# When a planned two-layer decoder trunk emits its weight loads, its reloads of x and the users of rows read back from DRAM

## The chip, the cores and the metric

The kernel runs on one core of one Trainium2 chip, as one program. The metric is the device time of one execution in microseconds (us); lower is better. Every time below is from the runs of the kernel before the change, or from one execution of it that the hardware profiler recorded.

## The reference

The reference is a decoder trunk of two layers over 256 positions of width 2048, all in float32. Each layer normalises its input, multiplies it by one wide input projection (`w_in`), feeds four groups of heads from the columns, gates each group, concatenates the four and multiplies by `w_out`; the result is added to x.

```python
h = rms_norm(x, norm_g)
p = split_columns(jnp.einsum("bsd,de->bse", h, w_in))
fox  = forgetting_attention(...) * silu(p["fox_g"])       # softmax with a cumulative forget bias
diff = rms_norm(differential_attention(...)) * silu(p["diff_g"])   # difference of two softmaxes
moba = moba_attention(...) * silu(p["moba_g"])            # at 256 positions: one causal block
gla  = rms_norm(gla_chunked(...)) * silu(p["gla_g"])      # gated linear attention
mixed = jnp.concatenate([fox, diff, moba, gla], axis=-1)
return x + jnp.einsum("bse,ed->bsd", mixed, w_out)
```

After the second layer comes one more rms_norm.

## The kernel before

**Products in parts.** Every weight tile is split into a high part (ScalarE, ACT, rounds it to the matmul's format) and a low part (VectorE, DVE, subtracts the high part from the raw tile). The activations are kept in two parts as well, `hTp` (layer input, transposed) and `mTh`, `mTl` (mixed rows, transposed). TensorE (PE) adds three products for each tile: high by high, low by high, high by low.

**Steps.** The work is a list of steps, `plan`. A plain step is two tiles of 128 rows by 512 columns, one raw load of 512 KB, and 12 matmuls; some blocks are 348 columns wide. Two of the input projections, `moba_v` and `diff_v`, are computed together in seven products of half size, the forms p1 to p7; their pair steps have 6 matmuls, and take a raw tile, or a tile `y` that lives in the buffer `xs` and is summed up in DRAM-to-SBUF transfers. `xs` holds x otherwise, so x is read back into it later, in four chunks of 512 columns: from the input in layer 0, from a copy in DRAM (`kept`) in layer 1. `X_AFTER` gives the steps after a layer's last pair step at which the four reloads are issued. The last pair step lies three steps into the block `diff_g`; `moba_g` follows with eight steps, and then `w_out`.

**Buffers.** There are five raw buffers and four for each of the high and low parts. A raw buffer is free when its low part has been computed.

**Order.** Nothing is scheduled by the hardware beyond the order in which instructions are written into each engine's queue, and semaphores. The order is made when the program is built, by a loop over the steps (lines 1706 to 1754). In each pass, for step i: results of finished blocks are taken (`settle`); `prepare(i + 3)` writes the high part of the step three ahead; the x reload stands here, if there is one; the matmuls of step i are written; `tick()` lets side tasks (attention, transposes, norms, written as generators) write some of their instructions; and `complete(i + 3)` writes the low part. The loads of raw tiles are written by `load_more()`, at the end of `prepare` and `complete`, as long as one of five buffers counts as free. Before the change a buffer counts as free as soon as its low part has been written into DVE's queue. The load itself carries the wait for that low part, and it stands in the queue of SyncE (SP), which issues in order.

**Estimates.** To decide when a side task may go on, the builder keeps a clock of its own, `times.now`, that the matmuls advance, and an estimated end for every tile. A task that yields goes on in a pass where the end of what it last wrote is at most `LEAD` = 1.5 us ahead of that clock; up to three such turns fit in one pass. Ends include a `HANDOVER` of 0.2 us. If a task yields a number, it goes on only when the clock has reached that end plus the number. These estimates decide order alone; at run time only the queues and semaphores count.

**Rows through DRAM.** A transposition of 128 x 1024 values is done in two moves, `turned`: DVE transposes 32 x 32 squares (STREAM_TRANSPOSE), SP writes the tile to DRAM in four transfers (`far<-four`, line 273), GpSimd (POOL) reads it back in another order (`four<-far`), and ACT copies it into place (`four<-four`). The estimate for the writes is `WRITE` = 5 us, for the read `READ` = 7.5. Queries, keys, probabilities and some gates go this way, and so do chunks of the layer input and the mixed rows of the groups `gla` and `diff` before `w_out`. In `w_out` the groups are used in the order gla, fox, diff, moba; PE's first step with diff rows is step 26 after the last pair step.

The lines that matter in the profile: L267 is any ACT or DVE instruction with an estimate, L273 a transfer with one, L442 a matmul, L1405 a raw load of a plain step, L1369 one of a pair step, L1366 a load of y, L1720 an x reload.

Of the kernel before, what the change touches and what calls it, by code (L numbers as in the profile page):

```python
# [34 lines left out]
RAW_BUFS = 5  # L35
PART_BUFS = 4
WARM = (512,) * 7 + (256,)
HALVED = 3
X_AFTER = (4, 10, 16, 22)
MIDDLE = ("gla_v", "fox_q", "fox_k", "fox_v", "fox_g", "diff_q", "diff_k", "moba_q", "moba_k", "diff_g", "moba_g", "moba_v", "diff_v")  # L40
NAMES = ("moba_v", "diff_v")
PAIR = tuple(3 + MIDDLE.index(z) for z in NAMES)
# [11 lines left out]
STALL = 0.3  # L54
LEAD = 1.5
HANDOVER = 0.2
SAFE = 1.0
ROOM = 2.0
BEFORE_LO = 1.5
# [190 lines left out]
class Timed:  # L250
# [5 lines left out]
    def __getattr__(self, name):  # L256
        f = getattr(self.eng, name)

        def call(*args, **kw):
# [4 lines left out]
            for a in (args[0], kw.get("accum_out")):  # L264
                if a is not None:
                    self.times.end(a, self.tail + HANDOVER)
            return f(*args, **kw)  # L267
# [72 lines left out]
def hybrid_trunk(  # L340
# [18 lines left out]
    times = Times()  # L359
# [23 lines left out]
    def take_side():  # L383
        yield SAFE
        return (yield from side.take([P, 1024]))

    def take_both():
        yield SAFE
        while len(side.free) < 2:
            yield  # L390
        return [side.get([P, 1024]) for _ in range(2)]
# [46 lines left out]
    def matmul(out, lhsT, rhs, start, stop, tiles=1, **kw):  # L438
        n = int(np.prod(rhs.shape[1:]))
        times.now += (n * 4 if lhsT.dtype == F32 else n + 32) / 2400.0 / tiles  # L440
        times.end(out, times.now + HANDOVER)
        t_.matmul(out, lhsT, rhs, start=start, stop=stop, **kw)  # L442

    def transpose(out, src):
        times.now += 0.109
        times.end(out, times.now + HANDOVER)
        t_.transpose(out, src, ident)
# [16 lines left out]
    def turned(pool, srcs, drop, what):  # L464


        x = sum(z.shape[2] for z in srcs)
        t = yield from pool.take([P, x * P])
        to, at = t.rearrange("p (j x r) -> p j x r", j=4, r=32), 0
        for z in srcs:  # L470
            v_.transpose(to[:, :, at:at + z.shape[2]], z)
            at += z.shape[2]
        drop()
        yield
        d = yield from far.take([4, 32, 4, x * 32])
        for i in range(4):
            q_.move(d[:, :, i].rearrange("j c f -> c j f"), t[32 * i:32 * i + 32].rearrange("c (j f) -> c j f", j=4), WRITE)
        yield
        g_.move(t, d.rearrange("j c i f -> (j c) (i f)"), READ)
        far.put(d)  # L480
        yield
        return t, t.rearrange("p (i x r) -> p x i r", i=4, r=32)

    def squares(rows):
# [863 lines left out]
    for i, s in enumerate(plan):  # L1348
        if "pair" in s:
            orders += [("y", i, None)] * (s["form"] == FORM_ORDER[0]) + [("raw", i, q) for q in s["from"]]  # L1350
        else:
            orders.append(("raw", i, None))
    loads = {"next": 0, "out": 0}

    def load_x(eng, a, b):
        if a % 4 == 0:
# [7 lines left out]
    def load_pair(kind, s, q):  # L1364
        if kind == "y":
            nc.sync.dma_start(ys[:, s["c"]], chunk_of(s, ("12", s["c"])))  # L1366
            return
        raw = wst.tile([P, STEP_W], F32, name="raw", bufs=RAW_BUFS).rearrange("p (j c) -> p j c", j=2)
        nc.sync.dma_start(raw, chunk_of(s, q))  # L1369
        s.setdefault("raws", []).append(raw)  # L1370

    def load_more():
        while loads["next"] < len(orders):
            kind, i, q = orders[loads["next"]]
            s = plan[i]
            if kind == "raw" and loads["out"] == RAW_BUFS:
                return
            if kind == "y" and s["pair"] and "kept" not in ready:
                return
            if "pair" in s:  # L1380
                load_pair(kind, s, q)
            else:
                load(i)
            loads["out"] += kind == "raw"
            loads["next"] += 1
            s["here"] = s.get("here", 0) + 1

# [145 lines left out]
    def rest_of_form(s):  # L1533
        l, f, c = s["pair"], s["form"], s["c"]
        y, raw = ys[:, c], s["raws"][0] if s["from"] else None
        lo_of(s["lo"], s["src"], s["hi"])
        if BY_DMA:
            q = {FORM_ORDER[0]: "11", "p5": "22", "p7": "21"}.get(f)
            if q:
                at = where[l, (q, c)]  # L1540
                g_.move(y, weights[at:at + P * 1024].rearrange("(p j c) -> p j c", p=P, j=2), 9.5, accum_op=OP.add)
        elif f == "p1":
            v_.tensor_add(y, y, raw)
        loads["out"] -= len(s["from"])

    def multiply_form(s):
        l, f, c = s["pair"], s["form"], s["c"]
# [84 lines left out]
    def prepare(i):  # L1632
        if i == 3:
            split_xt((2, 3))
        if 5 < i < 24 and i % 6 < 2:
            split_xt([i // 6 * 4 + i % 6 * 2 + k for k in range(2)])
        if i < len(plan):
            s = plan[i]
            while s.get("here", 0) < (len(s["from"]) + (s["form"] == FORM_ORDER[0]) if "pair" in s else 1):
                tick(False)  # L1640
                load_more()
            (form_parts if "pair" in s else parts_of)(s)
            soon = plan[i + 1] if i + 1 < len(plan) else {}
            if soon.get("form") == "p7" and "raws" in soon and "summed" not in soon:
                sum_early(soon)
        load_more()

    def complete(i):
        if i < len(plan):
            s = plan[i]  # L1650
            if "pair" in s:
                rest_of_form(s)
            else:
                if i >= HALVED:
                    lo_of(s["lo"], s["raw"], s["hi"])
                loads["out"] -= 1
            load_more()

    banks = {"next": deque(range(4)), "s": None}
# [1 line left out]
    def settle(waiting, bank=None):  # L1661

        tries = PATIENCE
        while waiting:
            if waiting[0]["key"] not in ready or len(s4.free) <= (KEPT if tries else 0):
                if bank is None or all(bank not in b["banks"] for b in waiting):
                    return
                tick(False)
                tries = max(tries - 1, 0)
                continue  # L1670
            b = waiting.popleft()
            times.latest = 0.0
            b["done"](results(b))
            if b["aside"]:
                side.put(b["side"])
# [8 lines left out]
    def lasts(z):  # L1684
        return 1.36 if "pair" in z else len(z["kts"]) * (z["block"]["n"] + 32) / 400.0
# [3 lines left out]
    last_of = {l: max(i for i, s in enumerate(plan) if s.get("pair") == l) for l in range(DEPTH)}  # L1689
    x_at = {last_of[l] + k: (l, c) for l in range(DEPTH) for c, k in enumerate(X_AFTER)}  # L1690
    load_more()
# [14 lines left out]
    for i, s in enumerate(plan):  # L1706
        if ("r", 0) not in ready:
            next(rms, None)
        while results_of:
            pair_result(results_of.popleft())  # L1710
        if banks["s"] is not None and "done" in pairs[banks["s"]]:
            banks["next"].append(pairs[banks["s"]]["bank"])
            banks["s"] = None
        settle(waiting)
        prepare(i + ahead)
        if i in x_at:
            l, k = x_at[i]
            c = slice(k * 512, k * 512 + 512)
            src = kept.rearrange("p (m d) -> p m d", m=2)[:, :, c] if l else x[0, :, c].rearrange("(m p) c -> p m c", p=P)
            nc.sync.dma_start(xs[:, :, c], src)  # L1720
        while not s["need"] <= ready.keys():
            tick(False)
        if "pair" in s:
            if s["form"] == FORM_ORDER[0] and s["first"]:
                k, ps = take_bank(False)
                pairs[s["pair"]] = {"bank": k, "ps": ps}
                banks["s"] = s["pair"]
            s["ps"] = pairs[s["pair"]]["ps"]
            multiply_form(s)
            if s["last"]:  # L1730
                results_of.append(s)
            if s["last"] and s["form"] in SUM_OF:
                given_out(("paired", s["pair"], SUM_OF[s["form"]]))
            if s["last"] and s["form"] == "p4":
                pairs[s["pair"]]["done"] = True
        else:
            b = s["block"]
            if s["first"]:
                b["banks"] = ()
                if b["aside"]:  # L1740
                    b["side"] = side.get([P, 1024])
                    b["ps"] = [b["side"][:, m * 512:m * 512 + 512] for m in range(2)]
                else:
                    b["banks"], b["ps"] = zip(*[take_bank() for _ in range(2)])
            multiply(s)
            if s["last"] and b["done"]:
                waiting.append(b)
        soon = sum(lasts(z) for z in plan[i + 1:i + ahead])
        ranks["v"] = min(AHEAD, soon - BEFORE_LO)
        ranks["a"] = min(AHEAD, soon - BEFORE_HI, ROOM if s["last"] else AHEAD)  # L1750
        tick()
        ranks["v"] = ranks["a"] = AHEAD
        complete(i + ahead)
    while tasks:
        tick(False)
    b = plan[-1]["block"]
# [31 lines left out]
```

## Time and profile before

| | |
|---|---|
| median of 3 runs | 908.04 us (906.04 to 908.85) |
| the profiled execution | 906.93 us, span 905.2 us |
| PE busy | 885.9 us (98%) |
| DVE busy | 662.6 us (73%) |
| ACT busy | 558.7 us (62%) |
| mean granted clock of PE | 0.995 |
| moved by DMA | 227.45 MB, mean 251 GB/s |
| raw loads of 512 KB | 271, median 5.3 us from issue to landing |

The profile shows each instruction with its engine and line, and for each idle stretch of an engine what ended it. "A <-B" after a duration is such a wait. The span runs from the first to the last instruction; busy time is the union of the instructions' times, and for PE it is modelled, so that a busy PE may still run at a reduced clock. "SPq" is SP's queue, which does nothing but issue transfers.

### The profile page before, as it was taken

Reading aid. Unit: us, or ns where it says so; the run is one execution under the profiler, and the core shown is the slowest. Engines: PE = TensorE matmul, PEld = TensorE weight load, DVE = VectorE, ACT = ScalarE, POOL = GpSimd, SP = SyncE. Lnnn points to the kernel's source line nnn. Section 1 sums busy time; section 2 is a strip of 40 time slices with the busy share of each in tenths; the row PEclk is TensorE's granted clock in tenths of the full one; section 3 lists DMA queues with packets and bytes.
Section 4 is the critical chain, followed back from the end, with each engine's and each line's share of the span. In section 5 each row is a group of like instructions: output and inputs, shape, how many; then the busy total and the mean of one; then the engine's idle time right before and its main releaser. Section 6 shows DMA issues by size and latency. Waiting matters only on the chain.

```text
span 905.2 us, 12467 instructions
## 1 busy us (share of the span) xinstructions
PE 885.9 (98%) x4380; PEld 752.4 (83%) x4380; DVE 662.6 (73%) x943; ACT 558.7 (62%) x846; POOL 60.4 (7%) x87
## 2 busy tenths in 40 slices
PE   9999999999999999989999989999999999999996
PEld 7988889888888888878899867898888888887786
DVE  6679988788677856657559947968767679565673
ACT  7567675587546658555746856657755466594561
POOL 1000110010010000000000010110001100001000
PEclk9999999999999999999999999999999999999999
DMA  8889997669797585968778997768959966859742
GB/s 295 277 264 309 257 303 234 225 193 317 231 290 243 192 296 191 321 229 249 253 242 297 292 324 199 217 194 287 290 213 272 290 215 200 303 180 352 267 153 94
DMA packets 84142, 227.45 MB, mean 251 GB/s; under 512 B 9979, under 2 KB 30443, under 8 KB 83950
## 3 DMA queue, kind: packets, MB, share of 16 engines
q1 hardware_dynamic: 73336, 192.00, 62.6%
q0 software_dynamic: 9152, 33.03, 14.0%
q10 hardware_dynamic: 1590, 1.62, 0.5%
q8 instruction: 34, 0.56, 0.2%
q14 instruction: 30, 0.25, 0.1%
HBM read 204.06 MB, written 22.55 MB: 250 GB/s over the span
## 4 chain that ended last, share of the span: by engine, by line
PE 81%; DMA 7%; DVE 5%; issue 5%; ACT 1%; POOL 0%; POOLq 0%; SPq 0%; ACTq 0%; DVEq 0%
PE mm L442 70%; PE side L442 11%; DMA four<-far 3%; DMA raw<-in_weights 2%; DVE lo L267 2%; DMA far<-four 1%; DVE four L267 1%; DVE mx L267 1%; DVE tq L267 0%; DVE mTl L267 0%; ACT hi L267 0%; ACT four L267 0%; ACT mTh L267 0%; DMA neg_b<-in_const_b 0%; DVE side L267 0%
## 5 line engine op out<-in xcount | busy, mean ns | idle before, releaser
L442 PE MATMUL mm<-hi,hTp 128*128 128x512 f32 (+1 forms) x1760 | 432.3, 382 | 3.7 <-ACT hi L267 3.1
L267 ACT ACTIVATE hi<-raw 128x1024 fp32r<-128x1024 f32 (+2 forms) x319 | 317.2, 1009 | 190.9 <-PE mm L442 110.6
L267 DVE TENSOR_TENSOR lo<-raw,hi 128x1024 fp32r<-128x1024 f32 (+2 forms) x319 | 363.3, 1155 | 94.0 <-ACT hi L267 87.6
L442 PEld LDWEIGHTS mm<-hi,hTp 128*128 128x128 f32 x1760 | 323.1, 188 | 64.1 <-ACT hi L267 4.3
L442 PE MATMUL mm<-lo,hTp 128*128 128x512 f32 (+1 forms) x880 | 237.9, 380 | 1.3 <-DVE lo L267 1.3
L442 PEld LDWEIGHTS mm<-lo,hTp 128*128 128x128 f32 x880 | 162.5, 188 | 33.1 <-DVE lo L267 3.4
L442 PE MATMUL mm<-hi,mTh 128*128 128x512 f32 (+1 forms) x256 | 70.0, 380 | 5.2 <-ACT mTh L267 5.2
L442 PE MATMUL mm<-lo,mTh 128*128 128x512 f32 (+1 forms) x256 | 69.7, 379 | 0.5 <-DVE lo L267 0.5
L442 PE MATMUL mm<-hi,mTl 128*128 128x512 f32 (+1 forms) x256 | 70.0, 381 | 0.1
L442 PEld LDWEIGHTS mm<-hi,mTh 128*128 128x128 f32 x256 | 45.8, 189 | 13.9 <-ACT mTh L267 6.0
L442 PEld LDWEIGHTS mm<-lo,mTh 128*128 128x128 f32 x256 | 46.6, 190 | 10.3 <-DVE lo L267 1.4
L442 PEld LDWEIGHTS mm<-hi,mTl 128*128 128x128 f32 x256 | 46.7, 190 | 9.7 <-DVE mTl L267 0.9
L267 ACT ACTIVATE four<-mm,rstd 128x512 f32<-128x512 f32 (+2 forms) x56 | 36.6, 669 | 25.1 <-PE mm L442 25.0
L273 POOL DMA_DIRECT2D four<-far x40 | 22.4, 559 | 406.2 <-DMA far<-four 175.1
L267 ACT ACTIVATE four<-four 128x512 fp32r<-128x512 f32 (+3 forms) x44 | 35.1, 820 | 18.2 <-DMA four<-far 18.1
L267 DVE STREAM_TRANSPOSE four<-four 128x1024 f32<-128x1024 f32 (+1 forms) x34 | 38.4, 1138 | 0.1
L442 PEld LDWEIGHTS side<-four,four 128*128 128x128 f32 (+1 forms) x336 | 36.3, 190 | 2.4 <-issue 1.4
L442 PE MATMUL side<-four,four 128*128 128x128 f32 (+3 forms) x336 | 37.2, 281 | 0.0
L273 POOL DMA_DIRECT2D xs<-in_weights x24 | 21.0, 875 | 208.5 <-DVE lo L267 55.0
L267 DVE TENSOR_TENSOR mTl<-four,mTh 128x1024 fp32r<-128x1024 f32 x16 | 19.5, 1220 | 17.7 <-ACT mTh L267 17.7
L267 ACT ACT_TABLE_LOAD x22 | 28.2, 1283 | 5.4 <-DVE nb L267 5.1
L267 DVE TENSOR_TENSOR four<-four,four 128x512 fp32r<-128x512 f32 (+3 forms) x31 | 26.6, 881 | 6.3 <-ACT four L267 6.3
(146 smaller groups left out, 679.2 us busy)
## 6 DMA issues: line engine op xcount, KB each, us to landing
raw<-in_weights SPq DMA_DIRECT2D x271, 512.0 KB, 5.3
four<-far POOLq DMA_DIRECT2D x34, 512.0 KB, 7.1
far<-four SPq DMA_DIRECT2D x128, 128.0 KB, 5.0
raw<-in_weights SPq DMA_DIRECT2D x46, 348.0 KB, 4.4
xs<-in_weights POOLq DMA_DIRECT2D x24, 512.0 KB, 7.6
xs<-in_weights SPq DMA_DIRECT2D x8, 512.0 KB, 7.9
xs<-in_x SPq DMA_DIRECT2D x4, 512.0 KB, 5.7
kept<-xs SPq DMA_DIRECT2D x1, 2048.0 KB
```

The lines of the kernel that those rows point to most:

```text
L267: return f(*args, **kw)
L273: self.eng.dma_start(out, src, **kw)
L442: t_.matmul(out, lhsT, rhs, start=start, stop=stop, **kw)
```

## The change

Three things are changed.

- **Loads.** `load_more` no longer takes a buffer as free when its low part is written, but when that low part's estimated end is at most `SOON` = 0.5 us ahead of the builder's clock. The ends wait in a queue, `loads["freed"]`. `load_more` is called at three more places of the loop: after `settle`, after the matmuls and before `tick`, and after `complete`. Where `prepare` needs a load that has not been written, it writes it at once (`urgent`).
- **Reloads of x.** `X_AFTER` goes from (4, 10, 16, 22) to (14, 18, 22, 26).
- **Rows from DRAM.** The last `yield` of `turned` becomes `yield LANDED`, with 0.01, so that the task goes on when the clock has reached the estimated landing.

```diff
-X_AFTER = (4, 10, 16, 22)
+X_AFTER = (14, 18, 22, 26)
...
+SOON = 0.5
+LANDED = 0.01
...
         g_.move(t, d.rearrange("j c i f -> (j c) (i f)"), READ)
         far.put(d)
-        yield
+        yield LANDED
...
-    loads = {"next": 0, "out": 0}
+    loads = {"next": 0, "out": 0, "freed": deque()}
...
-    def load_more():
+    def load_more(urgent=False):
+        by = math.inf if urgent else times.now + SOON
         while loads["next"] < len(orders):
             kind, i, q = orders[loads["next"]]
             s = plan[i]
-            if kind == "raw" and loads["out"] == RAW_BUFS:
+            if kind == "raw" and loads["out"] == RAW_BUFS and not (loads["freed"] and loads["freed"][0] <= by):
                 return
...
-            loads["out"] += kind == "raw"
+            if kind == "raw" and loads["out"] == RAW_BUFS:
+                loads["freed"].popleft()
+            else:
+                loads["out"] += kind == "raw"
...
     def rest_of_form(s):
...
-        loads["out"] -= len(s["from"])
+        loads["freed"].extend([times.of(s["lo"])] * len(s["from"]))
...
     def prepare(i):
...
                 tick(False)
-                load_more()
+                load_more(True)
...
     def complete(i):
...
-                loads["out"] -= 1
+                loads["freed"].append(times.of(s["lo"]))
             load_more()
...
         settle(waiting)
+        load_more()
         prepare(i + ahead)
...
             multiply(s)
             if s["last"] and b["done"]:
                 waiting.append(b)
+        load_more()
         soon = sum(lasts(z) for z in plan[i + 1:i + ahead])
...
         tick()
         ranks["v"] = ranks["a"] = AHEAD
         complete(i + ahead)
+        load_more()
```

## The prediction

> **What bounds the kernel now.** I read the page first, then the waits of TensorE, then windows around those waits, then the queues there.
>
> ```profile
> span 905.2 us, 12467 instructions
> PE 885.9 (98%) x4380; PEld 752.4 (83%) x4380; DVE 662.6 (73%) x943; ACT 558.7 (62%) x846; POOL 60.4 (7%) x87
> ```
>
> TensorE (PE) is busy for 98% of the span; the change alters no arithmetic, so only PE's idle time and its slow time can be won. The waits of PE (engine, line, what ended the wait: us in total, times, longest) say where:
>
> ```profile
> PE mm L442 <- ACT mTh L267: 5.2, 2, 2.9
> PE mm L442 <- ACT hi L267: 3.1, 1, 3.1
> PE mm L442 <- DVE lo L267: 1.8, 6, 0.4
> ```
>
> Ten microseconds in all, three waits making up 8.3. The windows (length, busy us and instructions of PE, PEld, DVE, ACT, POOL; granted clock; DMA share, GB/s) add what follows them:
>
> ```profile
> 370.00:380.00 10.00, 10.00 (x46) 8.29 (x45) 7.92 (x8) 4.86 (x7) 0.54 (x1) 1.00 1.03 370
> 392.00:394.00 2.00, 2.00 (x6) 1.52 (x6) 2.00 (x4) 2.00 (x4) 0.00 (x0) 0.54 0.36 119
> 530.00:540.00 10.00, 7.08 (x32) 5.53 (x30) 2.43 (x7) 2.92 (x3) 2.00 (x3) 1.00 1.04 367
> 542.00:544.00 2.00, 2.00 (x6) 1.52 (x6) 1.76 (x8) 2.00 (x4) 0.00 (x0) 0.50 0.71 248
> 550.00:560.00 10.00, 9.07 (x38) 6.47 (x37) 9.83 (x23) 5.87 (x8) 1.74 (x2) 1.00 0.66 160
> 840.00:850.00 10.00, 9.96 (x54) 8.63 (x55) 5.86 (x7) 5.80 (x7) 0.00 (x0) 1.00 0.87 328
> ```
>
> After the waits near 388 and 538 us the granted clock is about 0.5 for some 3.5 us (the rows at 392 and 542), which costs about 1.7 us each; after the third, near 837, it stays 1.00. So three places hold at most 8.3 + 3.4 us, plus about a microsecond of DVE-bound time at 550.
>
> **The change, part by part.** No instruction is added or removed; order in the queues changes. Part one, the loads: SP stands at a raw load, waiting for the low part that frees its buffer, for most of the kernel:
>
> ```profile
> SPq L1405 <- DVE lo L267: 527.4, 241, 8.6
> ```
>
> Whatever SP was given behind such a load waits too. Where only raw loads stand in the queue, emitting them later changes nothing: each still goes when its buffer is free. It matters only where row writes (far<-four, line 273) stand behind. Part three, `LANDED`: the ACT copy of rows read back from DRAM is emitted only at the estimated landing, not up to 1.5 us (`LEAD`) before, so more high parts go ahead of it on ACT. Where ACT waits for a late landing, nothing behind the copy is held that could have run; where the estimate was right, the consumer comes up to a step later.
>
> *Place A, 531 to 545 us (layer 1 begins).* PE, then ACT:
>
> ```profile
> 528.76 1.07 PE L442 MATMUL mm<-hi,hTp 128*128 128x512 f32 x4
> 530.12 1.98 PE L442 MATMUL mm<-hi,hTp 128*128 128x512 f32 x8
> 532.84 1.98 PE L442 MATMUL mm<-hi,hTp 128*128 128x512 f32 x8
> 535.56 1.07 PE L442 MATMUL mm<-hi,hTp 128*128 128x512 f32 x4
> 540.20 3.45 PE L442 MATMUL mm<-hi,hTp 128*128 128x512 f32 x8 [3.12 <-ACT hi L267]
> 544.65 1.99 PE L442 MATMUL mm<-hi,hTp 128*128 128x512 f32 x8
> ```
> ```profile
> 532.01 1.06 ACT L267 ACTIVATE hi<-raw 128x1024 fp32r<-128x1024 f32 x1 [4.14 <-DMA raw<-in_weights]
> 538.14 1.06 ACT L267 ACTIVATE four<-four 128x1024 f32<-128x1024 f32 x1 [5.07 <-DMA four<-far]
> 539.11 1.04 ACT L267 ACTIVATE hi<-raw 128x1024 fp32r<-128x1024 f32 x1
> 540.05 2.44 ACT L267 ACTIVATE four<-ct,dgs 128x128 f32<-128x128 f32 x8
> 542.39 2.00 ACT L267 ACTIVATE hi<-raw 128x1024 fp32r<-128x1024 f32 x2
> ```
>
> A plain step takes 532.84 to 535.56 = 2.72 us, a pair step half of it, so PE wanted the high part of 539.11 at 536.92 and began at 540.20: 3.28 us lost. The step then took 4.45 us (540.20 to 544.65), 1.73 over, the clock. ACT was not short of work: it stood behind the copy of 538.14. That copy was emitted between two high parts, in the pass that ends at PE's 530.12; that the pass before, at 528.76, did not emit it puts its estimated landing between 530.3 and 531.6 (1.5 us after each), so at 530.12 the new rule does not yet hold and the copy goes one step later, behind the high part of 539.11. Were that one's weights there? The rows on the way:
>
> ```profile
> 505.23 1.24 DVE L267 STREAM_TRANSPOSE four<-four 128x1024 f32<-128x1024 f32 x1
> 514.02 4.96 SPq L1405 DMA_DIRECT2D raw<-in_weights  x3
> 519.51 2.13 SPq L273 DMA_DIRECT2D far<-four  x4
> 523.83 4.57 SPq L1405 DMA_DIRECT2D raw<-in_weights  x3
> 531.33 0.55 POOL L273 DMA_DIRECT2D four<-far  x1 [9.97 <-DMA far<-four]
> ```
>
> They were issued by 523.83; even at the 11.8 us that the writes took (519.51 to 531.33) they land by 535.6, and the high part ends by 536.7. PE then starts at 536.92. The next high part follows the copy, 538.14 + 1.06 + 1.04 = 540.2, against 539.64 wanted; so that step begins near 540.2 instead of 544.65, a gain of 4.45, and with the eight small copies (2.44) ahead of the next high part some 3.8 is left a step later. Then it is given back in part: everything else behind the copy on ACT comes only one high part (1.05 us) earlier, and DVE, which from 541 on works off what ACT hands it (9.83 busy of 10 in the window at 550, PE 9.07), sets the pace. Ends: −5.0 (3.28 + 1.73, all kept) and +2.7 (a consumer one step late). Between the 1.05 that ACT surely passes on and 3.8, I take −2.0, nearer the ACT row because DVE follows ACT. That the writes go ahead of a raw load helps at most by the last load of the 514.02 row, about 1.5 us; I count nothing, since DVE's backlog also held back their emission.
>
> *Place B, the two layer ends.* The chain of waits with the timeline of layer 0, and below it layer 1:
>
> ```profile
> 360.28 16.35 PE mm L442 x72
> ...
> 379.32 8.19 DMA four<-far
> ```
> ```profile
> 367.40 1.24 DVE L267 STREAM_TRANSPOSE four<-four 128x1024 f32<-128x1024 f32 x1
> 367.55 3.14 SPq L1405 DMA_DIRECT2D raw<-in_weights  x2
> 369.10 2.37 DVE L267 TENSOR_TENSOR lo<-raw,hi 128x1024 fp32r<-128x1024 f32 x2 [0.46 <-ACT hi L267]
> 370.74 2.17 SPq L273 DMA_DIRECT2D far<-four  x4
> 389.82 1.57 PE L442 MATMUL mm<-hi,mTh 128*128 128x512 f32 x4 [2.31 <-ACT mTh L267]
> ```
> ```profile
> 819.84 2.27 SPq L273 DMA_DIRECT2D far<-four  x4
> 838.78 1.20 PE L442 MATMUL mm<-hi,mTh 128*128 128x512 f32 x4 [2.85 <-ACT mTh L267]
> ```
>
> The diff group's mixed rows are transposed by 368.64, but SP stands at the second load of the 367.55 row until its low part ends, about 370.3, and the writes start at 370.74: 2.1 us late, on the very chain (write, read 8.19, copy, high part) that PE waits for. Layer 1 repeats it. Does the new rule let the writes go first? Between two passes only the step's matmuls move the planner's clock (2.72); the load call behind them takes the load if its low part's estimated end lies within 2.72 + 0.5 = 3.22 us of the old pass; else the row writes, emitted next, precede it. From the transpose's start to that low part's end the trace has 2.94 us; `HANDOVER` adds 0.2; and that the writes were not emitted in the transpose's own pass says it started over 0.16 us after the planner's clock (1.34 + lag > 1.5). Sum 3.30 against 3.22: the writes go first, narrowly. Then they start 2.1 us earlier and the load about 0.5 us later, which its low part's three-step lead covers. What is late next is the read itself, so −2.1 of the 2.31 in layer 0 and −2.1 of the 2.85 in layer 1. Ends: layer 0 −4.0 (with the clock), layer 1 −2.85, and +2.7 each if the chain loses a step instead.
>
> On the clock, rows first: 0.54 after a wait of 2.31, 1.00 after one of 2.85. The Trainium skill, page "TensorE: Matmul & The Clock Gate", section "The HAM clock gate", says that the clock halves after an idle window of about 3.4 us that runs free of the program; no wait here is that long, so by the rule nothing would be won on the clock, by the row of 392 another 1.7. I count nothing.
>
> Part two, the x reloads: eight transfers of the same size, later on SP.
>
> ```profile
> 326.14 0.40 SPq L1720 DMA_DIRECT2D xs<-in_x  x1
> ...
> 343.57 1.06 ACT L267 ACTIVATE four<-four 128x1024 f32<-128x1024 f32 x1 [3.44 <-DMA four<-far]
> ...
> 345.12 2.84 PE L442 MATMUL side<-four,four 128*128 128x128 f32 x24
> ```
>
> The first stood ahead of the diff probabilities' writes; without it their read lands sooner and ACT's 3.44 us shrinks. But PE reached the product at 345.12 without waiting, so the order of PE's program sets it: cost and gain 0. The new places are steps 14, 18, 22 and 26, counted from the last pair step; step 26 is the one that PE waits for at 389.82, and the 360.28 row holds steps 16 to 21, so from about 354 to 390 there is one transfer more than before (at 16 and 22); ends −0.5 and +1.5 at place B (the issue, and 512 KB at the 370 GB/s of the 370 window), I take 0, since the row at 370 is as full either way.
>
> **Sum.** −2.0 − 2.1 − 2.1 = −6.2. The profiled execution took 906.93, so 900.7; the median of the runs, 908.04, is 1.1 above it, so 901.8.
>
> **The rivals.** *Nothing moves:* DMA share is 1.03 and 1.04 at the places, and order among transfers makes no bandwidth; then the reads land as late as now and only part of A is left, 0 to −2: 906 to 908. For it speaks the 11.8 us that the writes took; against it, that a load of 512 KB would stand behind 512 KB of writes and not ahead. The Trainium skill, page "DMA: Bandwidth & Descriptors", section "Issuing engines are not separate DMA queues", says that transfers of all issuing engines interleave on the same 16 DMA engines; by that only SP's 2.1 us of standing could be won, and at full share not even that. *Only one place gains:* A alone −2 to −4, or B alone −4.2: 904 to 906. *Slower:* `LANDED` delays the copy of 343.57 past one more step. Its product then comes 2.72 us later in PE's order, the diff rows with it, and both layer ends wait 2.7 us longer, with a second clock loss of 1.7: 5.4 + 1.7 − 2.0 = +5.1, so 913. It decides at an estimated landing later than the pass that now takes it, and 1.51 of a step's 2.72 is 0.55 were nothing known; but ACT's wait of 3.44 shows the estimate to be early, and the gain of 2.1 at place B would offset part of it.
>
> **How the numbers follow.** Both places gain: 0.42, 897 to 904 (either place by 2 us more or less). One place: 0.22, half of it beyond the 0.3% (2.7 us) that a measurement of this kernel can tell from no change. Nothing: 0.16. Slower: 0.20, a tenth of it offset to no change. So faster 0.55, same 0.26, slower 0.19. The range leaves 0.05 below (all ends of A and B at once, −11.5, 896.5) and some 0.13 above 911.
>
> **What would show it.** Right: ACT's order at place A has the copy behind one more high part and PE's wait there is under 1 us with the clock at 1.00; at the layer ends the writes start within 0.2 us of the transpose's end, ahead of the load, and PE waits below 1 us. SP's wait for low parts changes little in total. Wrong: the read at the layer ends is issued as late as now, or the product of 345.12 moves a step later; or new waits of PE for low parts near 550, where DVE has no room. It would also fail if copies emitted later left row buffers held so long that other tasks start late.

## The result, and the profile after

| kernel | median, us | lowest to highest | span of the profiled execution, us | mean granted clock |
|---|---|---|---|---|
| before | 907.04 | 903.87 to 908.85 | 905.2 | 0.995 |
| after | 895.81 | 895.38 to 896.36 | 893.6 | 0.998 |

The ratio is 0.988, with a 95% interval of 0.985 to 0.9911: 11 us, nearly twice the 6.2 us that the prediction summed to, and below its range.

First the page of the kernel after, span and busy time:

```profile
span 893.6 us, 12483 instructions
PE 881.4 (99%) x4380; PEld 751.4 (84%) x4380; DVE 662.7 (74%) x943; ACT 558.7 (63%) x846; POOL 60.4 (7%) x87
```

The same 4380 matmuls take 4.5 us less of busy time (885.9 before), 3.4 of them because two stretches at half clock, 3.4 us each, are gone, and PE is idle for 12.2 us instead of 19.3 (span less busy time). That is the 11.6 us of the span. The waits of PE after (engine, line, what ended the wait: total us, times, longest):

```profile
PE mm L444 <- DVE lo L269: 2.6, 5, 1.3
PE mm L444 <- ACT four L269: 1.4, 1, 1.4
```

The three waits of before (2.31, 3.12 and 2.85 us, for `mTh` twice and for `hi`) are gone; one of 1.4 us for an eviction (ACT takes a finished block from the matmuls' accumulators, `four<-mm`) and one of 1.3 for a low part are new. The windows (length, busy us and instructions of PE, PEld, DVE, ACT, POOL; granted clock; DMA share, GB/s) at the places of before:

```profile
370.00:380.00 10.00, 10.00 (x46) 8.29 (x45) 8.00 (x8) 5.25 (x7) 0.54 (x1) 1.00 1.02 378
392.00:394.00 2.00, 2.00 (x11) 1.65 (x10) 2.00 (x4) 1.16 (x2) 0.00 (x0) 1.00 0.89 263
530.00:540.00 10.00, 10.00 (x46) 8.29 (x45) 7.68 (x20) 8.12 (x15) 0.55 (x1) 1.00 1.04 362
542.00:544.00 2.00, 2.00 (x10) 1.67 (x9) 0.27 (x1) 1.99 (x4) 0.29 (x1) 1.00 0.53 61
```

PE is full in all four, the clock is 1.00 where it was 0.54 and 0.50, and the DMA share at 370 and 530 is as high as before: the transfers have no more room there.

The end of layer 0 in the timeline after (start, us, engine, line, operation, what it waited for), by queue: DVE, SP, POOL, ACT, PE, and below it two rows of the end of layer 1:

```profile
367.49 1.24 DVE L269 STREAM_TRANSPOSE four<-four 128x1024 f32<-128x1024 f32 x1
...
368.75 2.10 SPq L275 DMA_DIRECT2D far<-four  x4
370.95 1.41 SPq L1411 DMA_DIRECT2D raw<-in_weights  x2
...
377.16 0.54 POOL L275 DMA_DIRECT2D four<-far  x1 [11.64 <-PE mm L444]
...
384.38 1.15 ACT L269 ACTIVATE four<-four,dng 128x1024 f32<-128x1024 f32 x1 [3.92 <-DMA four<-far]
385.56 1.06 ACT L269 ACTIVATE mTh<-four 128x1024 fp32r<-128x1024 f32 x1
...
387.81 1.07 PE L444 MATMUL mm<-hi,mTh 128*128 128x512 f32 x4
```
```profile
809.11 2.10 SPq L275 DMA_DIRECT2D far<-four  x4
...
817.40 0.53 POOL L275 DMA_DIRECT2D four<-far  x1 [10.60 <-DMA far<-four]
```

The writes start at 368.75, 0.02 us after their transpose ends (367.49 + 1.24), and the raw load that stood ahead of them goes at 370.95, behind them. `mTh` is ready at 386.62, 1.2 us before PE wants it. The next lines show the place where layer 1 begins (SP, POOL, ACT, PE):

```profile
510.02 4.64 SPq L1411 DMA_DIRECT2D raw<-in_weights  x2
514.72 1.93 SPq L275 DMA_DIRECT2D far<-four  x4
516.74 0.42 SPq L1411 DMA_DIRECT2D raw<-in_weights  x1
517.20 0.50 SPq L1368 DMA_DIRECT2D xs<-in_weights  x1
...
522.11 0.55 POOL L275 DMA_DIRECT2D four<-far  x1 [5.28 <-DMA far<-four]
...
531.28 1.06 ACT L269 ACTIVATE hi<-raw 128x1024 fp32r<-128x1024 f32 x1 [0.20 <-DMA raw<-in_weights]
532.25 1.04 ACT L269 ACTIVATE four<-four 128x1024 f32<-128x1024 f32 x1
...
535.86 1.98 PE L444 MATMUL mm<-hi,hTp 128*128 128x512 f32 x8
```

Here two transfers of 512 KB that were ahead of the writes, a raw load and the `y` load (`xs<-in_weights`), are behind them. From the first write to the read's issue, which this document calls the way of the writes, it takes 7.4 us (514.72 to 522.11) instead of 11.8, and ACT's copy of 532.25 waits for nothing.

Comparing when the same matmul starts in both traces tells where the time came from (positive: after is ahead):

| stretch | change of the lead, us |
|---|---|
| start to 370 us | −0.5 |
| end of layer 0, 390 us | +4.2 |
| beginning of layer 1, 540 us | +5.2 |
| 619 to 637 us | −1.3 |
| end of layer 1, 838 us | +3.5 |

That is 11.1 of the 11.6 us; the rest lies in the rows behind the last of these matmuls. The first row is hardly the work of the change: two kernels below that hold none of its three parts, with `y` put later and with the row writes issued by POOL, are 0.8 and 1.7 us behind at 370 us as well.

### The profile page after: what moved, and what is told of

It reads as the page before. It is cut to its first block, busy times and chain, and to the rows that moved or that the text cites. A ratio compares the mean times of both kernels' runs of the same rounds, so it can differ in the third digit from the quotient of the medians.

```text
span 893.6 us, 12483 instructions
## 1 busy us (share of the span) xinstructions
PE 881.4 (99%) x4380; PEld 751.4 (84%) x4380; DVE 662.7 (74%) x943; ACT 558.7 (63%) x846; POOL 60.4 (7%) x87
## 4 chain that ended last, share of the span: by engine, by line
PE 92%; DVE 3%; DMA 1%; ACT 1%; issue 1%; POOLq 0%; POOL 0%; DVEq 0%; SPq 0%; ACTq 0%
PE mm L444 78%; PE side L444 14%; DVE lo L269 1%; DMA raw<-in_weights 1%; DVE mx L269 1%; DVE side L269 1%; ACT four L269 1%; DMA four<-in_xt 0%; DVE four L269 0%; ACT hi L269 0%; DVE tq L269 0%; ACT L269 0%; DVE mTl L269 0%; ACT mTh L269 0%; POOLq L1793 0%
## 5 line engine op out<-in xcount | busy, mean ns | idle before, releaser
L269 DVE TENSOR_TENSOR lo<-xs,hi 128x1024 fp32r<-128x1024 f32 x24 | 29.2, 1215 | 4.2 <-ACT hi L269 4.2
```

## Experiments: which part does it

Theory after the result: the loads' rule makes the whole gain, at each of the three places by putting one load behind the row writes. Rivals: `LANDED` makes the gain where layer 1 begins (540 us in the table); the x reloads, which leave the queue ahead of the layer ends, make the gain there; or the finer spacing of all loads does. The first kernels switch the three parts.

**The loads' rule alone**: the kernel after, without the other two parts.

```diff
-X_AFTER = (14, 18, 22, 26)
+X_AFTER = (4, 10, 16, 22)
...
-        yield LANDED
+        yield
```

> The load change alone (x reloads and row copies as before). Theory 1 (the order on SP makes the layer ends, the later copies make place A): the row writes start within 0.2 us of their transpose's end at both layer ends and PE's waits there go, 4.2 us in layer 0 and 3.5 in layer 1, while place A (layer 1's begin) keeps its wait of 3.1 us: about 899 us against 907. Rival 1 (the x reloads make the layer ends): the two waits stay, about 907. Rival 2 (place A is made by the row writes and their read coming earlier too): all three waits go, about 895.

Measured: 895.55 us, ratio 0.9862 (0.9823 to 0.9901). TensorE has no wait above 0.8 us:

```profile
PE mm L444 <- DVE lo L269: 2.7, 7, 0.8
```

All three waits are gone with this part alone, as its second rival had it; the lead grows by 4.3 at the end of layer 0, 4.3 where layer 1 begins and 3.5 at the end of layer 1.

**The x reloads alone**: the kernel before with the new `X_AFTER`.

```diff
-X_AFTER = (4, 10, 16, 22)
+X_AFTER = (14, 18, 22, 26)
```

> The x reloads alone (loads and row copies as before). Theory 1: nothing, 906 to 908, since PE's order sets the product of the diff rows, and SP still stands at the load ahead of the row writes at the layer ends. Rival 1: the layer ends gain 2 us or more each, 900 to 903.

Measured: 908.38 us, ratio 1.0001 (0.9981 to 1.002). All three waits stay (4.5 us for `mTh` in two, 3.5 for `hi`). The reloads neither help nor cost.

**LANDED alone**: the kernel before with the last `yield` of `turned` changed.

```diff
-        yield
+        yield LANDED
```

> The later row copies alone (loads and x reloads as before). Theory 1: place A gains 4 to 5 us because the copy on ACT stands behind one more high part, the layer ends keep 2.3 and 2.85 us: about 902. Rival 2: the read lands as late as before (about 6 us behind its estimate), so the copy still stands in front of the next high part and place A gains 2 us or less: 905 to 907. Slower, 910 or more, if the product of the diff rows slips by a step.

Measured: 906.13 us, ratio 0.9971 (0.9943 to 0.9999), barely a gain. Its timeline, ACT and then PE, and below it two rows of the kernel before:

```profile
535.37 1.06 ACT L268 ACTIVATE hi<-raw 128x1024 fp32r<-128x1024 f32 x1 [0.23 <-DMA raw<-in_weights]
539.96 1.06 ACT L268 ACTIVATE four<-four 128x1024 f32<-128x1024 f32 x1 [3.53 <-DMA four<-far]
...
635.79 1.15 ACT L268 ACTIVATE four<-four,gng 128x1024 f32<-128x1024 f32 x1 [1.51 <-DMA four<-far]
...
644.07 1.26 ACT L268 ACTIVATE four<-mm,rstd 128x512 f32<-128x512 f32 x2
```
```profile
540.50 1.98 PE L443 MATMUL mm<-hi,hTp 128*128 128x512 f32 x8
...
602.80 2.84 PE L443 MATMUL side<-four,four 128*128 128x128 f32 x24
...
624.33 2.49 PE L443 MATMUL side<-four,four 128*128 128x128 f32 x20
...
644.81 1.19 PE L443 MATMUL mm<-hi,hTp 128*128 128x512 f32 x4 [3.01 <-ACT four L268]
```
```profile
598.83 2.84 PE L442 MATMUL side<-four,four 128*128 128x128 f32 x24
...
618.26 2.49 PE L442 MATMUL side<-four,four 128*128 128x128 f32 x20
```

At 540 us the copy waits 3.53 us for its rows as before, but the high part that PE needs stands ahead of it, and PE goes on without a wait: 3.4 us are gained there. But the products of the heads now stand later in PE's program: at 602.80 and 624.33, where the kernel before has them at 598.83 and 618.26 though its PE is 3 us behind there. By the trace, what follows on them is late with them: the copy of 635.79 waits for its rows, ACT's work behind it pushes the evictions of 644.07 back, and PE stands 3.01 us for them. Of the 3.4 us won at 540, 2.9 are lost by 655.

**All but LANDED**, and **loads and LANDED, x as before**:

> All of the change but the later row copies. Theory 1: the layer ends gain as in the changed kernel, place A keeps a wait of about 3 us: about 900 against 895.8 for the whole change. Rival 2: place A gains as well, 895 to 897, and the later copies are worth nothing.

> The loads' rule and LANDED, with x reloaded where it was: with the four kernels measured, the table of the parts is nearly full. Theory (the loads' rule alone makes the gain, the parts do not help each other): 895 to 897.5 us, no wait of TensorE over 1 us at the layer ends and at 531 to 545 us; from LANDED about 1 us may be lost at 600 to 640 us, as one wait for an ACT copy. Rival (LANDED helps once the loads' rule is there): below 894.5. Rival (LANDED costs, and the x reloads made up for it in the changed kernel): 898 or more.

Measured: 896.9 us, ratio 0.9877 (0.983 to 0.9925), and 895.31 us, ratio 0.9866 (0.9844 to 0.9888). With the loads' rule in place neither other part moves the time by anything that these intervals tell. The 1.4 us wait of the kernel after is there with `LANDED` (1.40 us at 637.32 in the second) and absent without it.

## Experiments: which load, and where

The program's order shows that the loads' rule moves exactly one raw load behind the row writes at each place: before, 143, 201 and 303 raw loads stand ahead of the writes at the end of layer 0, the beginning of layer 1 and the end of layer 1; with the rule 142, 200 and 302. The lead `SOON` gives a way to move them one by one.

**SOON = 1.5 in the loads' rule alone** (142, 201, 302 raw loads ahead, so the new order at the layer ends only):

```diff
-SOON = 0.5
+SOON = 1.5
```

> The loads' rule with SOON = 1.5 in place of 0.5: at both layer ends the one load still goes behind the row writes, at 531 to 545 us it goes ahead of them again. Theory (each place hangs on the order of that one load): the waits at the layer ends stay away, some 3 us of wait and 1.7 us of halved clock come back at 531 to 545 us, so 899 to 902 us. Rival (the gain at 531 to 545 us comes from what the end of layer 0 won, or from the loads at large, not from the order there): 895 to 897 us. A second rival (the layer ends too need the shorter lead): 904 or more.

Measured: 898.94 us, just under the band, ratio 0.9905 (0.9881 to 0.9929). The longest wait of PE, and SP and POOL where layer 1 begins:

```profile
PE mm L444 <- ACT hi L269: 3.0, 1, 3.0
```
```profile
514.79 1.56 SPq L1411 DMA_DIRECT2D raw<-in_weights  x2
516.40 0.45 SPq L1368 DMA_DIRECT2D xs<-in_weights  x1
516.90 1.89 SPq L275 DMA_DIRECT2D far<-four  x4
...
528.33 0.56 POOL L275 DMA_DIRECT2D four<-far  x1 [10.43 <-DMA far<-four]
```

The layer ends keep their gain; where layer 1 begins the raw load and `y` are ahead of the writes, the read is issued 11.4 us after them, and the wait is back. That place does not live on what layer 0 won.

**The rule at that place alone** (143, 200, 303), in the loads' rule alone; `y_at` is the place of that `y` in the order of loads:

```diff
-        by = math.inf if urgent else times.now + SOON
+        by = math.inf if urgent or not y_at - 3 <= loads["next"] <= y_at + 5 else times.now + SOON
```

> The loads' rule in force for nine loads about the place at 515 to 525 us alone: there one raw load and the transfer y behind it go behind the row writes, all else in SP's queue stands as in the kernel before. Theory (the three places are independent and their gains add up): the wait of 3.1 us and the slow clock after it go, the waits of 2.3 and 2.9 us at the layer ends stay, 901 to 903.5 us beside 906 to 909 of the kernel before. Rival (the gain at this place is given back later, as with LANDED alone): 905 or more.

Measured: 904.39 us, ratio 0.9948 (0.993 to 0.9965).

```profile
PE mm L444 <- ACT mTh L269: 5.9, 2, 3.0
...
PE mm L444 <- ACT hi L269: 0.3, 1, 0.3
```

The wait for `hi` is gone and the two at the layer ends are there, as the theory had it, though the time is 0.9 us above its band. The profiled execution took 907.24 us, the longest of the five: its two waits are 0.7 us longer than before, and the clock after the second fell to 0.50, where the kernel before kept 1.00. By the ratios this place alone is worth 4.7 us and the layer ends alone 8.6, together 13.3; the whole rule alone measured 12.5, so they add up within the intervals.

**SOON = 2.0** (143, 201, 303: the order of before at all three):

> The loads' rule with SOON = 2.0: at all three places the raw load goes ahead of the row writes again, the new calls and the queue of ends stay. Theory (nothing but the order of that load counts): all three waits of TensorE are back, 904 to 909 us, same as the kernel before. Rival (the finer spacing of the other loads helps too): below 903.

Measured: 904.31 us, ratio 0.9963 (0.9941 to 0.9986). Its profile has the three waits back (5.0 us for `mTh` in two, 3.4 for `hi`) in a span of 907.0; this execution took 908.82 us, 4.5 above the median. Most of the gain goes with the order of three loads, but not all: the interval lies wholly below 1, so 0.1 to 0.6 per cent stay with the order of before. Whether they come from the spacing of the other loads or from something else that the new calls move, these runs do not tell.

**What makes the writes slow where layer 1 begins.** There two transfers changed sides. Two kernels move one each: the loads' rule alone with `y` put one place earlier, so that only the raw load goes behind the writes, and the kernel before with `y` put one place later, so that only `y` does.

```diff
+    orders[y_at - 1:y_at + 1] = orders[y_at], orders[y_at - 1]
```
```diff
+    orders[y_at:y_at + 2] = orders[y_at + 1], orders[y_at]
```

> The loads' rule, with one transfer y (512 KB, layer 1, the fourth) put one place earlier, so that at 515 us it goes ahead of the row writes, and only the raw load goes behind them. Theory (every 512 KB ahead of the writes makes them land later, by 512 KB at some 250 to 370 GB/s = 1.4 to 2.1 us): the writes take 8 to 9.5 us from the first issue to landing instead of 7.2, TensorE waits 0 to 1.5 us there, 895.5 to 898 us. Rival (only SP standing at the raw load for its buffer counts, not what is ahead in the DMA queues): the writes take 7 to 7.5 us, 895 to 896.5. Rival (y is what made the writes late): they take 10 us or more, the wait of 3 us is back, 899 or more.

> The kernel before with that one transfer y put one place later, so that it goes behind the row writes; the raw load that SP stands at stays ahead of them, and so does all else. Theory (bytes ahead count, each 512 KB 1.4 to 2.1 us): the writes start 0.5 us earlier and take 9 to 9.8 us instead of 11.2, TensorE's wait there falls from 3.1 to between 0.5 and 1.5 us, the layer ends stay: 902.5 to 906 us. Rival (only the standing counts): wait 2.5 to 3.1, 905 to 909. Rival (y alone made it late): no wait there, 901 to 903.

Measured: 900.44 us, ratio 0.9907 (0.9889 to 0.9925), and 906.71 us, ratio 0.9985 (0.9971 to 1.0). SP, POOL and PE's wait in the first, then in the second:

```profile
517.25 2.06 SPq L275 DMA_DIRECT2D far<-four  x4
...
528.49 0.55 POOL L275 DMA_DIRECT2D four<-far  x1 [8.23 <-DMA far<-four]
```
```profile
PE mm L444 <- ACT hi L269: 2.7, 1, 2.7
```
```profile
520.35 2.40 SPq L273 DMA_DIRECT2D far<-four  x4
...
531.32 0.55 POOL L273 DMA_DIRECT2D four<-far  x1 [10.32 <-DMA far<-cum]
```
```profile
540.39 2.11 PE L442 MATMUL mm<-hi,hTp 128*128 128x512 f32 x8 [2.00 <-ACT hi L267]
```

In the second the profile puts the end of the read's wait down to `far<-cum`, a small transfer; in the trace's semaphore records the last of the four writes lands in the same moment, at 530.61, and that is what the read needs. Both expectations of a cost of 1.4 to 2.1 us for each 512 KB fell. The first came out as its rival that `y` made the writes late, but the second, where `y` is behind them, is nearly as slow. With `y` alone ahead the way of the writes is 11.2 us, with the raw load alone ahead 11.0, with both 11.8 and 11.4 (before, and SOON = 1.5). Either one is enough to bring most of the wait back. With neither ahead it is 9.6 us in the kernel with the rule at this place alone, and 7.4, 7.8, 9.2 and 9.3 in the four kernels with the whole rule (after; the rule alone; all but `LANDED`; loads and `LANDED`). So what is queued in front counts, and SP's standing at the load is not the whole of it (with `y` alone ahead, the raw load that SP had stood at is behind the writes). But the order of these two does not give the way by itself: with one order it spreads over 2 us, and in the kernel with `LANDED` alone, where both of them and one more raw load are ahead, it is 9.8 us (523.50 to 533.27). How the transfers in flight share their time is not settled by these runs.

## Experiments: the same order by other means

**Row writes issued by POOL**, the loads as before:

```diff
-            q_.move(d[:, :, i]..., t[...]..., WRITE)
+            g_.move(d[:, :, i]..., t[...]..., WRITE)
```

> The kernel before with its row writes issued from GpSimd's queue, which issues the reads too, in place of SP's; the loads stay as and when they were. Theory (SP standing at a load for its buffer holds the writes): the writes start within 0.3 us of their transposes' end, the reads at the layer ends come 2 us earlier or more and the waits there go: 895 to 899 us. Rival (the bandwidth that the load takes, not the standing, makes the writes late): writes start early but take 2 us longer, the reads come as late as before: 904 to 908. If GpSimd's queue now stands at the writes and holds reads behind it, ACT's waits for rows grow: 907 or more.

Measured: 896.97 us, ratio 0.9881 (0.9853 to 0.9909). Its timeline, DVE, then POOL:

```profile
368.74 1.24 DVE L267 STREAM_TRANSPOSE four<-four 128x1024 f32<-128x1024 f32 x1
...
370.27 2.20 POOL L273 DMA_DIRECT2D far<-four  x4 [0.77 <-DVE four L267]
...
509.22 2.57 POOL L273 DMA_DIRECT2D far<-four  x4
```

No load changes its place in SP's queue, yet the result is nearly the kernel after. At the end of layer 0 the writes go 0.29 us after their transpose (369.98). Where layer 1 begins they go at 509.22, while SP had them at 519.51 (PE is 0.9 us ahead of the kernel before there); that is not within the expected 0.3 us of the transpose, which ends at 505.60, for POOL stood at a transfer of its own into `xs`. A wait of 1.0 us for `mTh` is left, and the rival is part of the reason: relative to PE the writes of 370.27 start 2.2 us earlier than before, but their way is 10.4 us (to the read of 380.71) instead of 8.6, so the read goes only 0.3 us earlier. The three places gain 2.6, 4.2 and 3.5 us of lead. The loads need not be moved at all: getting the writes out of the queue in which they stood behind the loads is enough.

**A rule without estimates**, in the kernel before: no raw load while a transposed tile is unwritten (`unwritten` is filled in `turned` after the transpose and emptied before its writes are issued). As in the change, `prepare` writes a load that it needs at once (`urgent`), and `load_more` is called once more after `complete`.

```diff
-            if kind == "raw" and loads["out"] == RAW_BUFS:
+            if kind == "raw" and (loads["out"] == RAW_BUFS or unwritten and not urgent):
```

> The kernel before with one rule and no estimate: no raw load is written while a transposed tile has not been written to DRAM yet. Where SP has no such tile, loads go out as before. Theory (only the order of a row write and the load beside it matters): 894 to 898 us, waits for low parts in SP's queue of the same total within 15 us, the three waits of TensorE gone. Rival (the loads' spread over the step, as the estimate makes it, is what helps, by spacing the transfers): 903 to 908 us. If holding loads back starves the high parts, new waits of ACT for raw appear and TensorE waits for hi: 905 or more.

Measured: 897.69 us, ratio 0.9889 (0.9859 to 0.992); a wait of 1.3 us for `hi` is left. SP's waits for low parts fall by 19 us in total (584.0 before, lines 1405 and 1369 together), a little more than the 15 expected. Most of the gain comes with the order, without the estimated ends.

## Why the prediction was wrong

**The bound** was right: the three waits and the slow clock after two of them were where the time lay, 8.3 + 3.4 us. The three places gave 12.9 us of lead and the span became 11.6 shorter; the prediction took "all ends of A and B at once, −11.5" (its ends add up to −11.85: 5.0, 4.0 and 2.85) for what lies below its range, with a chance of 0.05. Of its sum of −6.2, place A gave 5.2 in place of 2.0 and place B 7.7 in place of 4.2; 1.3 us were lost at 619 to 637, where it had no term.

**Place A is the step that failed.** "That the writes go ahead of a raw load helps at most by the last load of the 514.02 row, about 1.5 us; I count nothing, since DVE's backlog also held back their emission." The writes went ahead of that load and of `y`, and relative to PE the read landed some 5.1 us earlier (by PE's matmuls, after is 3.8 us ahead there): 1.0 from the earlier start, 4.4 from the shorter way of the writes, −0.3 from the read. That makes the 3.12 us wait and the 1.7 us of slow clock vanish whole. With the rule at this place alone the way is 2.2 us shorter, not 4.4 (9.6 instead of 11.8), and that is enough; where the other 2.2 come from stays open. Nor was it DVE that held the writes: their transpose ended at 506.47 before (505.23 + 1.24), SP issued them at 519.51, and from POOL they went 9.4 us earlier relative to PE. The gain was put on `LANDED` instead. The mechanism of `LANDED` was read rightly: alone, it puts one more high part ahead of the copy and wins 3.4 us at this place. In the kernel after the copy too stands behind that high part, but the read is so early that the order is of no weight, and the loads' rule without `LANDED` gains as much over all.

**"It is given back in part", near 550,** did not come: one wait of 1.32 us for a low part against three of 0.93 together before. What came of it came 90 us later, at 637, 1.4 us in the kernel after and 3.01 with `LANDED` alone.

**Place B** had the right mechanism and the wrong size. The writes do precede the load, 2.0 us earlier at 368.75; but "What is late next is the read itself" counted the read at 8.19 us, and it took 7.2 (377.16 to the copy's 384.38). The copies of layer 1, before and after:

```profile
836.49 1.15 ACT L267 ACTIVATE four<-four,dng 128x1024 f32<-128x1024 f32 x1 [6.72 <-DMA four<-far]
```
```profile
824.53 1.15 ACT L269 ACTIVATE four<-four,dng 128x1024 f32<-128x1024 f32 x1 [3.72 <-DMA four<-far]
```

PE is 7.6 us ahead there, so these rows were there some 4.4 us earlier relative to PE; those of layer 0, where PE is 0.5 us behind, some 3.6, and not 2.1; each wait went whole. In both layers the earlier start of the writes and the shorter read made the gain; the way of the writes changed by 0.6 us at most. The gains are 4.2 and 3.5 us where 2.1 each was counted, beyond even the ends of 4.0 and 2.85.

**The clock was counted as nothing at place B**, though the row at 392 stood at 0.54; it went to 1.00 with the wait, 1.7 us. By the section "The HAM clock gate" of the Trainium skill's page "TensorE: Matmul & The Clock Gate" no wait of the kernel before was long enough for that (it asks for some 3.4 us); the row measured decides against the rule as it was applied there, to the wait's length alone.

**"Sum 3.30 against 3.22: the writes go first, narrowly"** was false precision. At the layer ends the writes still went first at SOON = 1.5 and no longer at 2.0, so the margin was a microsecond or more, and the chance for place B should have been larger. The chances as listed add up to 0.53 for faster, 0.29 for the same and 0.18 for slower, not quite to the 0.55, 0.26 and 0.19 given; nothing else hangs on that.

**Part two at 0** was right (1.0001). SP's waits for low parts fell little, as said (527.4 us before on the line of plain loads), and the writes now wait for their transposes in SP's queue:

```profile
SPq L1411 <- DVE lo L269: 518.8, 242, 9.3
...
SPq L275 <- DVE four L269: 24.3, 24, 2.8
```

**The rivals.** "Order among transfers makes no bandwidth" holds at place A (367 GB/s in the window at 530 before, 362 after) and is beside the point: at a DMA share of 1.04 the order decided which transfer was served early, and the raw loads had a slack that the writes had not: in the kernel after, PE waits for no high part. The prediction drew from the section "Issuing engines are not separate DMA queues" of the Trainium skill's page "DMA: Bandwidth & Descriptors" that no more than SP's standing could be won at full share; that was too much to draw from it, for at place A a shorter way of the writes gave 4.4 us, and 2.2 with the order changed there alone. The kernel with POOL's writes agrees with the section that another issuing engine brings no other lanes: the writes of 509.22 had landed by 521.16, after 11.9 us, no faster than the 11.2 from SP before (519.51 to 530.67). "Slower" named a real mechanism, a product that `LANDED` puts later in PE's order, but at 345 us, where nothing moved; it came at 600 to 645 us, with waits of 1.4 (after) and 3.0 us (`LANDED` alone), not with 5 or more.

## What to carry to other kernels

A queue that issues in order and stands at waits is a schedule of its own: ask, for each transfer on the chain that the bottleneck waits for, what stands ahead of it that has slack, and move that behind it; here one load at each of three places, at one of them with the transfer `y` behind it, was worth 11 us, and issuing the transfer from another queue was worth nearly the same. The gain from the order is not the time that the queue stood: where layer 1 begins the writes started 1.0 us earlier and their way became 4.4 us shorter, at the layer ends the earlier start and the read behind it made the gain. And a wait that ends a chain should be costed whole, with the slow clock that may follow, and a chain that gets a little earlier at its head should not be assumed to keep its other lengths.

## What the runs showed of the hardware

The granted clock after a wait of PE is not told by the wait's length. Rows of the kernel with `LANDED` alone (a wait of PE, then two windows: length, busy us and matmuls of PE, granted clock, DMA share, GB/s), and a window of the kernel with `y` put later:

```profile
390.21 1.72 PE L443 MATMUL mm<-hi,mTh 128*128 128x512 f32 x4 [1.96 <-ACT mTh L268]
```
```profile
392.00:394.00 2.00, 2.00 (x6) 0.50 0.22 29
646.00:648.00 2.00, 2.00 (x11) 1.00 0.03 8
```
```profile
544.00:546.00 2.00, 2.00 (x10) 1.00 0.40 137
```

A wait of 1.96 us was followed by 0.50, one of 3.01 (at 644.81) by 1.00, and one of 2.00 (at 540.39 in the second kernel) by 1.00. Of the 19 waits between 1.9 and 3.6 us in these profiles, the clock fell to half during or right after 14; the five after which it stayed were of 2.00, 2.35, 2.75, 2.85 and 3.01 us. The half clock lasted 3.4 us in eleven cases and 6.8 in three (waits of 3.02, 3.05 and 3.53 us), so a wait of this size cost its own length and, 14 times in 19, another 1.7 or 3.4 us. It also differs from execution to execution of one kernel: of 46 executions of the kernel before, the 15 with a mean granted clock of 0.992 or less have a median of 909.95 us, the 8 with 0.996 or more one of 906.29.
